# A planned one-core decoder block: a margin in the planner's costs, a later lower-bound computation, another order of filler columns

## The chip, the cores and the metric

The kernel runs on one core of a Trainium2 chip. The metric is the device time of one execution in microseconds. Beside the runs there is one profiled execution, whose trace gives every time quoted here unless a sentence says otherwise. The engines are called PE (matrix products), DVE (VectorE), ACT (ScalarE), POOL (GpSimd) and SP (it issues most DMAs).

## The reference

One decoder block on a 1024 x 1024 float32 activation, cut to what matters here:

```python
xn = rms_norm(x, norm1_g)
q, k, v, hq, hf, hi, hg, gate_sb, gate_hg = split(xn @ w_in)     # 1024 x 5632
o_sb = stick_breaking_attention(rms(q), rms(k), v)               # 8 heads of 64
f    = lb + (1 - lb) * sigmoid(hf)                               # lb: softmax of lb_table
o_hg = rms(hgrn2(silu(hq), f, hi)) * silu(hg)                    # 4 heads of 128
h    = x + (sigmoid(gate_sb) * (o_sb @ wb0) + sigmoid(gate_hg) * (o_hg @ wb1)) @ w_out
out  = h + (silu(rms(h) @ w_gate) * (rms(h) @ w_up)) @ w_down
```

Stick-breaking attention needs a reversed running sum of softplus over each row of scores; HGRN2 needs a running sum of log f and a decayed product between all pairs of rows. `lb` is a softmax over two rows of a table, 512 channels.

## The kernel before, in words

Activations lie transposed, channels on partitions, in two halves of 512 tokens. Products run at float32 accuracy on a reduced-precision path: each operand is split into a rounded part and a remainder (`ah`/`al` for activations, `oh`/`ol` for weights, `th`/`tl` for others), and three matmuls replace one. The rounded part is a copy on ACT or POOL, the remainder a subtraction on DVE.

The first stage computes the input projections and everything up to the branch outputs. There are four **units**: unit u is attention head pair u (`scores`, `values`) and HGRN head u (`hgrn`). A unit needs seven columns of 128 from `w_in` (q, k, v, hf, hq, hi, hg); sixteen more columns, called G, are the branch gates and wait for nobody. One column is 2 halves x 8 channel tiles x 3 = 48 matmuls of 128x512. The string list `FILL` says in which order the columns after the first six are projected while units 0 to 3 are worked on: a letter G is a gate column, `a` is the q, k, v of the next unit, the others are HGRN columns.

The order of nearly all instructions comes from a list scheduler inside the kernel, the class `Plan`. Every operation is recorded with a cost in us (`A` for ACT, `V` for DVE, `G` for POOL, `M` and `T` for PE, `L` for loads on SP), the operations it depends on and the buffers that it needs; `issue()` then plays the recorded operations on a clock of its own and writes them out, engine by engine, in the order in which they would start. A result can be used `max(FROM[producer], TO[consumer])` us after its producer's planned end, 0.14 us where no entry stands. `plan.at` gives a planned time before which an operation doesn't start. Projections have rank -1: they fill whatever PE time nothing else wants. On the chip each engine executes its own list strictly in the order written and waits on semaphores, so a wrong cost shows as a wait.

A score tile `z` is written by PE, then read by a chain on ACT (Abs, Relu, Exp, Ln into `aa` and `ww`) and DVE (a scan into `aa`, a subtraction into `ww`), after which its bank (two of them) is free for the next score tile. `vx` holds v, transposed on PE once DVE has scaled it. In `hgrn`, `kb` are key, running sum and the product matrix, `dl` the decayed operands of one level, and `sums` splits its operand on POOL (`th`) and DVE (`tl`) before PE sums it.

Names and lines of the kernel before: `setup` at L288 computes `lb` outside the planner; the first loads stand at L357 to L360; `WARM` matmuls on a constant at L378 run ahead of the first real ones; all planned instructions carry L204, the line at which `issue()` calls them, so they are told apart by their tiles. The output-branch, output and FFN stages that follow are planned too, with PE's order fixed by a chain; the last product (L1209) is written by hand.

Of the kernel before, what the change touches and what calls it, by code (L numbers as in the profile page):

```python
# [10 lines left out]
F32 = mybir.dt.float32  # L11
# [9 lines left out]
P = 128  # L21
# [8 lines left out]
LEVELS = [64, 32, 16, 8, 4, 2, 1]  # L30
FILL = ["GgGGaifq", "gGaGfiqGG", "gaGGGiqGfGG", "gGGG"]
BANKS = [3, 2, 3]
WARM = 9
ORDER = [1, 6, 2, 5, 7, 4, 3]
# [49 lines left out]
class Plan:  # L84
# [140 lines left out]
def hybrid_block(ctx: ExitStack, tc, xT, wi, wb, wo, wg, wu, wd, vec, outT):  # L225
# [62 lines left out]
    def setup(sp):  # L288
        make_identity(nc, ident)
        t2 = sp.tile([P, P], F32, tag="t2", name="t2")  # L290
        nc.vector.memset(t2, 0.0)
        nc.vector.memset(t2[0:64, 0:64], 1.0)
        nc.vector.memset(t2[64:128, 64:128], 1.0)
        nc.vector.tensor_copy(bones_r, t2)
        nc.vector.memset(never, NEG)

        for f, base, step in ((future[0], 0, -1), (future[1], 1 - P, 1)):
            nc.gpsimd.memset(f, 1.0)
            nc.gpsimd.affine_select(out=f, in_=f, pattern=[[1, P]], compare_op=ALU.is_ge, fill=0.0,
                                    base=base, channel_multiplier=step)  # L300
        nc.vector.tensor_scalar(qg, vt[:, V_Q:V_Q + 1], 0.125, None, op0=ALU.mult)
        l0, l1 = vt[:, V_LB:V_LB + 4], vt[:, V_LB + 4:V_LB + 8]
        mx = sp.tile([P, 4], F32, tag="mx", name="mx")
        e0 = sp.tile([P, 4], F32, tag="e0", name="e0")
        e1 = sp.tile([P, 4], F32, tag="e1", name="e1")
        nc.vector.tensor_tensor(mx, l0, l1, op=ALU.max)
        nc.vector.tensor_tensor(e0, l0, mx, op=ALU.subtract)
        nc.vector.tensor_tensor(e1, l1, mx, op=ALU.subtract)
        nc.scalar.activation(e0, e0, AF.Exp)
        nc.scalar.activation(e1, e1, AF.Exp)  # L310
        nc.vector.tensor_tensor(e1, e0, e1, op=ALU.add)
        nc.vector.reciprocal(e1, e1)
        nc.vector.tensor_tensor(lb, e0, e1, op=ALU.mult)
        nc.vector.tensor_scalar(omlb, lb, -1.0, 1.0, op0=ALU.mult, op1=ALU.add)
        nc.vector.tensor_scalar(nomlb, omlb, -1.0, None, op0=ALU.mult)

# [42 lines left out]
    nc.sync.dma_start(vt, vec)  # L359
    nc.sync.dma_start(first_w[0][0], first_src[0][:, :256])  # L360
    nc.scalar.preload_act_table_set("natural_log_exp_and_others")
# [90 lines left out]
    def fixed(tile):  # L452
        return Buf(None, lambda: tile)

    def A(fn, *args, n=HALF, aps=0, rank=0, ps=False, part=False, holds=(), after=(), **kw):
        us = (0.05 if ps else 0.093) + n / 1200 + 0.0935 * aps
        return plan.op("A", us, [(fn, args, kw)], rank, after, part=part, holds=holds)

    def V(fn, *args, n=HALF, aps=0, rank=0, part=False, holds=(), after=(), **kw):
        cycles = 2 * n if fn == nc.vector.tensor_tensor_scan else n  # L460
        us = 0.067 + cycles / 960 + 0.061 * aps
        return plan.op("V", us, [(fn, args, kw)], rank, after, part=part, holds=holds)

# [42 lines left out]
    def pool_copy(dst, src, rank=0, after=(), holds=()):  # L506
        return G(nc.gpsimd.tensor_scalar, dst, src, 1.0, 0.0, op0=ALU.mult, op1=ALU.add, us=0.68,
                 rank=rank, after=after, holds=holds)

    lvl_mask = []  # L510

    def level_masks():
# [5 lines left out]
        apart = fixed(apart)  # L518
        V(tt, apart, row, column, op=ALU.bitwise_xor, n=2 * P)
        for m in LEVELS:  # L520
# [28 lines left out]
    def first_piece(pieces, u, i):  # L549

        cut, src = slice(256 * i, 256 * i + 256), fixed(first_w[u][i])
        if i:
            load(src, first_src[u][:, cut], 128)
            hi, lo = (Buf(None, lambda b=b: b.buf.tile) for b in pieces[0])
            op = A(nc.scalar.copy, hi[:, cut], src, n=256, rank=2, holds=pieces[0])
        else:
            hi, lo = new("oh", dt=F32R), new("ol", dt=F32R)
            op = V(nc.vector.tensor_copy, hi[:, cut], src, n=128, rank=3)
            plan.at[op] = 2.3 + 0.3 * u
        V(tt, lo[:, cut], src, hi[:, cut].bitcast(F32), op=ALU.subtract, n=256, rank=3 - i)  # L560
        pieces.append((hi, lo))

    def take_x(h):
# [4 lines left out]
        for k in range(KT):  # L568
# [17 lines left out]
            if h == k == 0:  # L586
                plan.at[op] = 1.9
            V(stt, xl[k][h][:, hs(h)], x, g, xh[k][h][:, hs(h)].bitcast(F32), op0=ALU.mult,
              op1=ALU.subtract, aps=1, rank=2 - h)
            if k == 0:  # L590
                plan.at[A(act, acc, x, AF.Square, rank=1 - h)] = 1.9
            else:
                sq = new("ww")
                A(act, sq, x, AF.Square, rank=1 - h)
                sqs.append(sq)
# [8 lines left out]
    def proj(ws, h, after=None, ring="pj"):  # L604

        pss = [new(ring) for _ in ws]
        for k in range(KT):
# [693 lines left out]
```

## Time and profile before

| what | us |
|---|---|
| median of 3 runs (1499.06 to 1499.98) | 1499.16 |
| the profiled execution | 1496.39 |
| its span, first to last instruction | 1494.7 |
| PE busy | 1479.0 |
| DVE busy | 1193.1 |
| ACT busy | 806.5 |
| POOL busy | 92.3 |

A matmul's row shows 0.39 us from start to modelled end, though the next one starts 0.23 us after it: matmuls overlap. PE's busy time is the union of such rows, and a wait appears as idle time only where the previous row has ended. The time from the end of the span to the end of the execution, and what lies ahead of the span, is 1496.39 - 1494.7 = 1.69 us.

### The profile page before, as it was taken

What the parts mean: (1) busy time and instruction counts of PE and PEld (TensorE: products, weight loads), DVE (VectorE), ACT (ScalarE), POOL (GpSimd) and SP (SyncE); (2) the same over time, 40 slices, a digit from 0 to 9 for tenths busy, and PEclk for the clock granted to TensorE, in tenths of its full rate; (3) what the DMA queues carried; (4) which work ended last, traced back from release to release, by engine and by line L of the source; (5) the groups of instructions that cost most, each with busy time, mean ns of one, the idle gap of its engine ahead of it and who ended that gap; (6) DMA issues with size and microseconds to landing.
All of it is one profiled execution on the core that took longest, in us unless ns stands there. A gap on an engine that the chain in (4) does not pass through costs nothing.

```text
span 1494.7 us, 20135 instructions
## 1 busy us (share of the span) xinstructions
PE 1479.0 (99%) x7021; PEld 1224.2 (82%) x7021; DVE 1193.1 (80%) x2114; ACT 806.5 (54%) x1515; POOL 92.3 (6%) x131
## 2 busy tenths in 40 slices
PE   9999999999999999999999999999999999999999
PEld 7778888788878888888888888888888888888887
DVE  8899779988998678978867798888888888585553
ACT  8866868668757788546434453333333333354442
POOL 1111101211111001110000000000000000000000
PEclk9999999999999999999999999999999999999999
DMA  5011111111111211217434245444444445797662
GB/s 198 29 59 52 57 47 33 56 45 56 53 46 45 76 48 48 74 66 266 166 113 161 101 157 173 163 166 160 165 167 168 169 167 170 265 328 228 195 223 87
DMA packets 83445, 188.50 MB, mean 126 GB/s; under 512 B 9616, under 2 KB 12176, under 8 KB 83344
## 3 DMA queue, kind: packets, MB, share of 16 engines
q1 hardware_dynamic: 72688, 167.95, 33.7%
q10 hardware_dynamic: 10656, 19.27, 3.5%
q8 instruction: 55, 0.90, 0.2%
q14 instruction: 46, 0.38, 0.1%
HBM read 131.61 MB, written 55.57 MB: 125 GB/s over the span
## 4 chain that ended last, share of the span: by engine, by line
PE 81%; DVE 11%; ACT 5%; issue 2%; DMA 1%; POOL 1%; SPq 0%; POOLq 0%; DVEq 0%; ACTq 0%
PE pj L204 35%; PE ms L204 19%; PE f L1209 14%; PE z L204 13%; DVE dl L204 2%; DVE aa L204 2%; ACT aa L204 2%; DVE kb L204 1%; DVE ol L204 1%; DVE tail L204 1%; DVE tl L204 1%; ACT ww L204 1%; DVE ww L204 1%; ACT xf L204 1%; ACT qhh L204 0%
## 5 line engine op out<-in xcount | busy, mean ns | idle before, releaser
L204 PE MATMUL pj<-ah,oh 128*128 128x512 f32 x696 | 283.1, 407 | 0.5 <-DVE oh L204 0.5
L204 PE MATMUL pj<-ah,ol 128*128 128x512 f32 x696 | 272.7, 392 | 0.0
L204 PE MATMUL pj<-al,oh 128*128 128x512 f32 x696 | 271.9, 391 | 0.4 <-DVE al L204 0.3
L204 ACT CAST oh<-w 128x512 fp32r<-128x512 f32 x168 | 101.6, 620 | 236.0 <-PE ms L204 83.5
L204 DVE TENSOR_TENSOR ol<-w,oh 128x512 fp32r<-128x512 f32 x248 | 167.4, 690 | 10.6 <-ACT oh L204 8.3
L204 PE MATMUL ms<-f,oh 128*128 128x512 f32 x528 | 162.6, 389 | 0.2 <-DVE g L204 0.2
L204 PEld LDWEIGHTS pj<-ah,ol 128*128 128x128 f32 x696 | 130.6, 188 | 29.1 <-DVE ol L204 0.2
L204 PEld LDWEIGHTS pj<-al,oh 128*128 128x128 f32 x696 | 131.1, 189 | 23.6 <-DVE al L204 1.8
L204 PEld LDWEIGHTS pj<-ah,oh 128*128 128x128 f32 x696 | 131.2, 188 | 22.5 <-ACT ah L204 1.4
L204 PEld LDWEIGHTS ms<-f,oh 128*128 128x128 f32 x528 | 99.0, 188 | 21.1 <-DVE g L204 0.6
L1209 PE MATMUL f<-bl,ah 128*128 128x512 f32 x296 | 115.3, 389 | 0.0
L1209 PE MATMUL f<-bh,ah 128*128 128x512 f32 x296 | 115.2, 389 | 0.0
L1209 PE MATMUL f<-bh,al 128*128 128x512 f32 x296 | 115.2, 389 | 0.0
L204 DVE TENSOR_TENSOR_SCAN aa<-aa,ww 128x128 f32<-128x128 f32 (+3 forms) x96 | 93.7, 990 | 26.7 <-ACT aa L204 19.8
L204 PE MATMUL z<-f,oh 128*128 128x512 f32 x352 | 108.4, 389 | 0.0
L204 PE MATMUL pj<-f,oh 128*128 128x512 f32 x352 | 108.4, 389 | 0.0
L257 DVE TENSOR_TENSOR al<-ra,ah 128x512 fp32r<-128x512 f32 x73 | 50.5, 691 | 71.3 <-ACT ah L256 71.3
L204 PE MATMUL ms<-f,ol 128*128 128x512 f32 x264 | 102.7, 389 | 0.0
L256 ACT CAST ah<-ra 128x512 fp32r<-128x512 f32 x73 | 45.4, 622 | 94.6 <-PE f L1209 82.2
L204 POOL TENSOR_SCALAR oh<-w 128x512 fp32r<-128x512 f32 x80 | 64.4, 807 | 380.6 <-PE pj L204 311.9
L204 PE MATMUL pj<-mx,oh 128*128 128x512 f32 x256 | 78.8, 389 | 0.0
L204 PEld LDWEIGHTS pj<-f,oh 128*128 128x128 f32 x352 | 66.1, 188 | 13.6
(266 smaller groups left out, 3125.4 us busy)
## 6 DMA issues: line engine op xcount, KB each, us to landing
w<-wi SPq DMA_DIRECT2D x42, 512.0 KB, 3.6
rb<-act_d SPq DMA_DIRECT2D x73, 256.0 KB, 4.2
w<-wg SPq DMA_DIRECT2D x22, 512.0 KB, 3.6
w<-wu SPq DMA_DIRECT2D x22, 512.0 KB, 3.9
w<-wd SPq DMA_DIRECT2D x22, 512.0 KB, 4.7
wd_d<-ds SPq DMA_DIRECT2D x44, 256.0 KB, 2.7
ra<-wd_d SPq DMA_DIRECT2D x44, 256.0 KB, 4.0
act_d<-c SPq DMA_DIRECT2D x40, 256.0 KB, 4.5
```

The lines of the kernel that those rows point to most:

```text
L204: fn(*[a.real() if isinstance(a, View) else a for a in args], **{k: v.real() if isinstance(v, View) else v for k, v in kw.items()})
L256: pin(nc.scalar.copy(hi, src))
L257: pin(nc.vector.tensor_tensor(lo, src, hi.bitcast(F32), op=ALU.subtract))
L1209: nc.tensor.matmul(banks[SET[o]][d], l[:, ws], r, start=start and i == 0, stop=p == NP - 1 and i == 2, skip_group_check=True)
```

## The change

Five edits. (1) The planned cost of every ACT and DVE operation is multiplied by 1.02. (2) A result of POOL counts as usable 0.5 us after its planned end instead of 0.14, and POOL may start 0.24 us after its producer instead of 0.14. (3) The columns come in another order: with `a` as three, the four strings of `FILL` held 10, 11, 13 and 4 columns and now hold 11, 11, 10 and 6; there are sixteen G in both. (4) The ten small operations that compute `lb`, `omlb` and `nomlb` go from the hand-written beginning into the plan, with planned time 45 or later, and the operation that makes `apart` (for the level masks) gets planned time 40. (5) At the beginning, the load of the first weights becomes the first load of the plan, the rounded copy of the second column's first weights goes from DVE to ACT, there are 7 constant matmuls instead of 9, and the first matmuls are grouped otherwise.

```diff
-FILL = ["GgGGaifq", "gGaGfiqGG", "gaGGGiqGfGG", "gGGG"]
+FILL = ["GGgGaifqG", "gGaGGfiqG", "gaGiqGfG", "GgGGGG"]
-WARM = 9
+WARM = 7
-    FROM = {"P": 0.2, "D": 2.0}
-    TO = {"P": 0.35}
+    FROM = {"P": 0.2, "D": 2.0, "G": 0.5}
+    TO = {"P": 0.35, "G": 0.24}
...
-        l0, l1 = vt[:, V_LB:V_LB + 4], vt[:, V_LB + 4:V_LB + 8]
-        mx = sp.tile([P, 4], F32, tag="mx", name="mx")
...
-    nc.sync.dma_start(first_w[0][0], first_src[0][:, :256])
...
+    MARGIN = 1.02
     def A(fn, *args, n=HALF, aps=0, rank=0, ps=False, part=False, holds=(), after=(), **kw):
         us = (0.05 if ps else 0.093) + n / 1200 + 0.0935 * aps
-        return plan.op("A", us, [(fn, args, kw)], rank, after, part=part, holds=holds)
+        return plan.op("A", us * MARGIN, [(fn, args, kw)], rank, after, part=part, holds=holds)
...
-        return plan.op("V", us, [(fn, args, kw)], rank, after, part=part, holds=holds)
+        return plan.op("V", us * MARGIN, [(fn, args, kw)], rank, after, part=part, holds=holds)
...
+    lb, omlb, nomlb = (fixed(t) for t in (lb, omlb, nomlb))
+    def lower_bounds():
+        l0, l1 = vt[:, V_LB:V_LB + 4], vt[:, V_LB + 4:V_LB + 8]
+        plan.at[V(tt, omlb, l0, l1, op=ALU.max, n=4)] = 45.0
+        V(tt, lb, l0, omlb, op=ALU.subtract, n=4)
+        V(tt, nomlb, l1, omlb, op=ALU.subtract, n=4)
+        A(act, lb, lb, AF.Exp, n=4)
+        A(act, nomlb, nomlb, AF.Exp, n=4)
+        V(tt, omlb, lb, nomlb, op=ALU.add, n=4)
+        V(nc.vector.reciprocal, omlb, omlb, n=4)
+        V(tt, lb, lb, omlb, op=ALU.mult, n=4)
+        V(ts, omlb, lb, -1.0, 1.0, op0=ALU.mult, op1=ALU.add, n=4)
+        V(ts, nomlb, omlb, -1.0, None, op0=ALU.mult, n=4)
...
-        V(tt, apart, row, column, op=ALU.bitwise_xor, n=2 * P)
+        plan.at[V(tt, apart, row, column, op=ALU.bitwise_xor, n=2 * P)] = 40.0
...
+        if i or u == 0:
+            load(src, first_src[u][:, cut], 128)
         if i:
-            load(src, first_src[u][:, cut], 128)
...
-            op = V(nc.vector.tensor_copy, hi[:, cut], src, n=128, rank=3)
-            plan.at[op] = 2.3 + 0.3 * u
+            if u:
+                plan.at[A(nc.scalar.copy, hi[:, cut], src, n=256, rank=3)] = 2.6
+            else:
+                V(nc.vector.tensor_copy, hi[:, cut], src, n=128, rank=3)
...
-                groups = [a[:2] + b[:2], a[2:] + b[2:]]
+                groups = [a[:2], b[:1], a[2:] + b[2:], b[1:2]]
```

The new costs redraw the list of the whole first stage; what follows shows the written order at three places. In the names, a number behind a tile is its buffer; they differ between the two programs without meaning.

The first place is the beginning on DVE: the lower bounds (`mx` to `nomlb`), the mask operand `apart` and the first weights' rounded copies `oh`. Before:

```order
L301 TENSOR_SCALAR qg_89<-vt_66 128x1
L306 TENSOR_TENSOR mx_205<-vt_66 128x4
L307 TENSOR_TENSOR e0_206<-vt_66,mx_205 128x4
L308 TENSOR_TENSOR e1_207<-vt_66,mx_205 128x4
L311 TENSOR_TENSOR e1_207<-e0_206,e1_207 128x4
L312 RECIPROCAL e1_207<-e1_207 128x4
L313 TENSOR_TENSOR lb_90<-e0_206,e1_207 128x4
L314 TENSOR_SCALAR omlb_91<-lb_90 128x4
L315 TENSOR_SCALAR nomlb_92<-omlb_91 128x4
L204 TENSOR_TENSOR apart_243<-tmp_257,tmp_255 128x256
L204 CAST oh_265<-kb_177 128x256
L204 CAST oh_271<-kb_178 128x256
```

Now:

```order
L301 TENSOR_SCALAR qg_89<-vt_66 128x1
L204 CAST oh_249<-kb_177 128x256
L204 SCALAR_TENSOR_TENSOR al0_156<-tail_179,vt_66,ah0_155 128x512
L204 TENSOR_TENSOR ol_258<-kb_177,oh_249 128x256
L204 TENSOR_TENSOR ol_263<-kb_178,oh_251 128x256
L204 SCALAR_TENSOR_TENSOR al1_158<-aa_242,vt_66,ah1_157 128x512
```

Nine operations left the front of the first weights' copy, and one copy went to ACT.

The second place is on PE, where unit 0's v (`vx`) is transposed between the tiles of a projection. Before:

```order
L204 MATMUL pj_649<-ah5_165,oh_536 128x512
L204 MATMUL pj_649<-al5_166,oh_536 128x512
L204 MATMUL pj_649<-ah5_165,ol_544 128x512
L204 MATMUL ms_703<-ident_81,vx_607 128x128 x4
L204 MATMUL ms_710<-ident_81,vx_607 128x128 x4
L204 MATMUL pj_649<-ah6_167,oh_536 128x512
L204 MATMUL pj_649<-al6_168,oh_536 128x512
L204 MATMUL pj_649<-ah6_167,ol_544 128x512
```

Now:

```order
L204 MATMUL pj_634<-ah5_165,oh_520 128x512
L204 MATMUL pj_634<-al5_166,oh_520 128x512
L204 MATMUL pj_634<-ah5_165,ol_530 128x512
L204 MATMUL pj_634<-ah6_167,oh_520 128x512
L204 MATMUL pj_634<-al6_168,oh_520 128x512
L204 MATMUL pj_634<-ah6_167,ol_530 128x512
L204 MATMUL ms_696<-ident_81,vx_591 128x128 x4
L204 MATMUL ms_705<-ident_81,vx_591 128x128 x4
```

The transposes stand three matmuls later.

The third place is on DVE in unit 1's `hgrn`: `kb` (the product of key and query) is copied by POOL into `th`, and `tl` is the remainder, which waits for that copy. Before:

```order
L204 TENSOR_TENSOR xq_2755<-tmp_2790,xq_2755 128x512
L204 TENSOR_TENSOR ww_2783<-z_2731,aa_2835 128x512
L204 TENSOR_TENSOR kb_2869<-kb_2664,xq_2755 128x512
L204 TENSOR_TENSOR dl_2746<-xq_2755,dl_2746 128x256
L204 TENSOR_TENSOR dl_2761<-xq_2755,dl_2761 128x256
L204 TENSOR_TENSOR dl_2746<-dl_2746,kb_2664 128x2x2x64
L204 TENSOR_TENSOR tl_2892<-kb_2869,th_2880 128x512
```

Now, with the row that writes this `kb` (kb_2805) eight rows above the first one shown:

```order
L204 SCALAR_TENSOR_TENSOR aa_2851<-aa_2720,ww_2819 128x512
L204 SCALAR_TENSOR_TENSOR tmp_2828<-xq_2817,tmp_2828 128x512
L204 SCALAR_TENSOR_TENSOR aa_2866<-aa_2651,aa_2646,ww_2821 128x512
L204 TENSOR_TENSOR xq_2817<-tmp_2828,xq_2817 128x512
L204 TENSOR_TENSOR ww_2821<-z_2642,aa_2866 128x512
L204 TENSOR_TENSOR tl_2884<-ms_2784,th_2795 128x512
L204 TENSOR_TENSOR ww_2819<-z_2667,aa_2851 128x512
L204 TENSOR_TENSOR tl_2896<-ms_2808,th_2835 128x384
L204 TENSOR_TENSOR tail_2781<-tail_2781,xq_2740 128x512
L204 COPY_PREDICATED z_2900<-future0_84,never_86 128x128
L204 COPY state_2918<-ms_2904 128x128
L204 TENSOR_TENSOR tl_2925<-kb_2805,th_2909 128x512
```

Three operations stood between `kb` and its `tl`; now there are eighteen. Over the first stage's eight such pairs the mean goes from four to six, and for the last level's eight sums (`tl<-dl`) from two to four. From the output-branch stage on, PE's order is the same in both programs.

More of the change, by code (lines that the diff above doesn't have):

```diff
@@ L301, in setup @@
         nc.vector.tensor_scalar(qg, vt[:, V_Q:V_Q + 1], 0.125, None, op0=ALU.mult)
-        l0, l1 = vt[:, V_LB:V_LB + 4], vt[:, V_LB + 4:V_LB + 8]
-        mx = sp.tile([P, 4], F32, tag="mx", name="mx")
[L304 to L315, printed above, removed]
     COL = {"q": 0, "k": 4, "v": 8, "hq": 12, "hf": 16, "hi": 20, "hg": 24, "G": 28}
@@ L551, in first_piece @@
         cut, src = slice(256 * i, 256 * i + 256), fixed(first_w[u][i])
+        if i or u == 0:
+            load(src, first_src[u][:, cut], 128)
         if i:
-            load(src, first_src[u][:, cut], 128)
             hi, lo = (Buf(None, lambda b=b: b.buf.tile) for b in pieces[0])
-            op = A(nc.scalar.copy, hi[:, cut], src, n=256, rank=2, holds=pieces[0])
+            A(nc.scalar.copy, hi[:, cut], src, n=256, rank=2, holds=pieces[0])
         else:
             hi, lo = new("oh", dt=F32R), new("ol", dt=F32R)
-            op = V(nc.vector.tensor_copy, hi[:, cut], src, n=128, rank=3)
-            plan.at[op] = 2.3 + 0.3 * u
+            if u:
+                plan.at[A(nc.scalar.copy, hi[:, cut], src, n=256, rank=3)] = 2.6
+            else:
+                V(nc.vector.tensor_copy, hi[:, cut], src, n=128, rank=3)
         V(tt, lo[:, cut], src, hi[:, cut].bitcast(F32), op=ALU.subtract, n=256, rank=3 - i)
@@ L586, in take_x @@
             if h == k == 0:
-                plan.at[op] = 1.9
+                plan.at[op] = 2.0
             V(stt, xl[k][h][:, hs(h)], x, g, xh[k][h][:, hs(h)].bitcast(F32), op0=ALU.mult,
@@ L590, in take_x @@
             if k == 0:
-                plan.at[A(act, acc, x, AF.Square, rank=1 - h)] = 1.9
+                plan.at[A(act, acc, x, AF.Square, rank=1 - h)] = 2.1
             else:
@@ L899, in hybrid_block @@
             take_x(1)
+            lower_bounds()
             level_masks()
```

## The prediction

> **What bounds the kernel now.** I read the page's busy shares first, then the windows by stage, then who made PE wait, then the timeline around three of those waits.
>
> ```profile
> span 1494.7 us, 20135 instructions
> PE 1479.0 (99%) x7021; PEld 1224.2 (82%) x7021; DVE 1193.1 (80%) x2114; ACT 806.5 (54%) x1515; POOL 92.3 (6%) x131
> ```
>
> PE is the bound: 15.7 us of the span are left beside its busy time. A window's row gives, after the stretch and its length, each engine's busy time; PE comes first, then weight loads, DVE, ACT, POOL.
>
> ```profile
> 0.00:10.00 10.00, 8.04 (x23) 5.36 (x23) 6.95 (x29) 6.73 (x13) 4.02 (x15) 1.00 0.80 267
> 10.00:50.00 40.00, 39.23 (x171) 30.90 (x170) 36.89 (x62) 36.20 (x64) 1.92 (x2) 1.00 0.34 119
> 50.00:250.00 200.00, 198.07 (x1023) 165.45 (x1024) 173.10 (x338) 155.69 (x325) 27.84 (x37) 1.00 0.16 50
> 250.00:450.00 200.00, 195.10 (x1029) 162.19 (x1028) 178.79 (x365) 137.00 (x276) 31.51 (x39) 1.00 0.16 49
> 450.00:690.00 240.00, 237.90 (x1256) 199.81 (x1255) 188.64 (x344) 172.46 (x349) 27.05 (x39) 1.00 0.24 83
> 690.00:1490.00 800.00, 799.71 (x3522) 660.06 (x3521) 608.03 (x979) 298.45 (x492) 0.00 (x0) 1.00 0.52 176
> ```
>
> PE stands idle 1.96 us in the first 10, 0.77 to 50, then 1.93, 4.90 and 2.10 us, 8.93 in all from 50 to 690. After 690 it is 0.29 us in 800. So only the first stage has anything to give, and its worst stretch is the one where DVE is fullest (178.79 of 200). Who ended the waits:
>
> ```profile
> PE z L204 <- DVE ww L204: 3.4, 5, 1.1
> PE ms L204 <- DVE kb L204: 2.9, 6, 0.8
> PE ms L378 <- DVE ones_r L365: 1.4, 1, 1.4
> PE ms L204 <- DVE vx L204: 1.0, 1, 1.0
> PE ms L204 <- DVE tl L204: 0.8, 2, 0.5
> PE ms L204 <- DVE ot L204: 0.4, 1, 0.4
> PE ms L204 <- ACT ww L204: 0.4, 1, 0.4
> ```
>
> Nearly all are DVE being late by a few tenths, 16 waits of some 0.55 us in these rows from 50 on. The largest:
>
> ```profile
> 431.69 0.39 PE L204 MATMUL pj<-al,oh 128*128 128x512 f32 x1
> 431.92 0.39 PE L204 MATMUL pj<-ah,ol 128*128 128x512 f32 x1
> 433.42 0.50 PE L204 MATMUL z<-khl,qhh 128*128 128x512 f32 x1 [1.11 <-DVE ww L204]
> ```
>
> Matmuls follow each other by 0.23 us, so this one was due at 432.15 and started 1.27 late: the idle time shown, 1.11, hides 0.16 more, since the row of the one before runs on to its modelled end. The 16 waits therefore cost about 8.9 + 16 x 0.16 = 11.5 us.
>
> **The beginning (edits 4 and 5).**
>
> ```profile
> 3.08 0.23 DVE L306 TENSOR_TENSOR mx<-vt 128x4 f32<-128x4 f32 x1
> 5.33 0.42 DVE L204 TENSOR_TENSOR apart<-tmp 128x256 int32<-128x256 int32 x1
> 5.70 0.50 DVE L204 CAST oh<-kb 128x256 fp32r<-128x256 f32 x2
> 1.72 0.42 SPq L360 DMA_DIRECT2D kb<-wi  x1
> 6.14 0.54 PE L204 MATMUL pj<-ah,oh 128*128 128x512 f32 x1 [0.48 <-DVE oh L204]
> 6.58 0.50 PE L204 MATMUL pj<-ah,ol 128*128 128x512 f32 x1
> L378 PE MATMUL ms<-ones_r 128*128 128x512 f32 x9 | 4.2, 647 | 1.4 <-DVE ones_r L365 1.4
> ```
>
> From 3.08 to 5.7 DVE works on the lower bounds and the mask, and the copy that PE waits for stands behind them. With these gone, the weights themselves decide; the copy has no idle time before it, so they had landed by 5.7. Their load is issued third on SP, behind 256 KB of x; at the 267 GB/s of the first window those 256 KB take 1.0 us, so as first load its data come about that much earlier, near 4.7, and x a half us later, 128 KB. Nine constant matmuls take 4.2 us, seven some 3.3 and end near 4.8. The first real one can start at about 5.0 instead of 6.14: 1.1 us. [...]
>
> Not all of it lasts, since DVE and ACT are 92% and 90% busy from 10 to 50:
>
> ```profile
> 15.97 1.32 ACT L204 ACTIVATE ah<-xf,vt 128x512 fp32r<-128x512 f32 x2
> 17.36 0.74 DVE L204 SCALAR_TENSOR_TENSOR al<-xf,vt,ah 128x512 fp32r<-128x512 f32 x1
> 19.43 0.51 PE L204 MATMUL pj<-al,oh 128*128 128x512 f32 x1 [0.29 <-DVE al L204]
> ```
>
> ACT's work here follows loads that the change doesn't hasten, so the first `ah<-xf` stays near 16.0 and ends near 16.6; its `al` can start 0.7 earlier than 17.36 at best. PE, 1.1 ahead, waits 0.4 more at 19.43: I keep 0.7. Ten small operations come back near 45 us, at 0.16 each about 1.3 us of DVE, beside masks and under projections; three of them stand ahead of the last `vx` piece:
>
> ```profile
> 50.53 0.44 PE L204 MATMUL ms<-ident,vx 128*128 128x128 f32 x2 [0.97 <-DVE vx L204]
> ```
>
> The transposes moved three matmuls back, 0.68 us, and DVE has 0.3 to 0.5 more ahead of `vx`: 0.2 of this wait goes. Together -0.9; bounds +0.5 (the x tile's half us decides) and -2.1 (1.1 kept, all of the 0.97 gone).
>
> **The costs (edits 1 and 2).** How wrong were the planner's costs? It charges a 512-wide subtraction 0.067 + 512/960 = 0.600 us, and a projection's three matmuls 1536/2255 + 0.009 = 0.690.
>
> ```profile
> 29.34 0.69 DVE L204 TENSOR_TENSOR tl<-aa,th 128x512 fp32r<-128x512 f32 x1
> 29.94 0.69 DVE L204 TENSOR_TENSOR tail<-tail,ww 128x512 f32<-128x512 f32 x1
> ```
>
> DVE starts one every 0.60, as charged. PE does three in 0.68 (431.69 to 431.92 is 0.23 each), 1.3% faster than charged. So over a stretch in which DVE has no pause, PE runs ahead of the plan and meets a DVE that is on time for the plan, late for PE. A DVE cost 2% higher lets it be late by 2% of such a stretch: over 10 to 15 us, 0.2 to 0.3. Taking 0.25 from each of 16 waits of 0.72 gives 4.0 at most; short waits have less to give, so 3.3.
>
> Other lateness comes from POOL:
>
> ```profile
> 249.35 1.33 POOL L204 TENSOR_SCALAR th<-kb 128x512 fp32r<-128x512 f32 x1 [4.39 <-PE z L204]
> 249.79 0.42 DVE L204 TENSOR_TENSOR dl<-dl,kb 128x256 f32<-128x256 f32 x1
> 250.72 0.69 DVE L204 TENSOR_TENSOR tl<-kb,th 128x512 fp32r<-128x512 f32 x1 [0.51 <-POOL th L204]
> 255.42 0.71 PE L204 MATMUL ms<-dl 128*128 128x128 f32 x4 [0.65 <-DVE kb L204]
> ```
>
> DVE stood 0.51 for a POOL copy and PE waited 0.65 five us later. The planner charges that copy 0.07 + 512/840 = 0.68 us; it took 1.33. With 0.36 more allowed for, DVE's `tl` stands eighteen operations behind `kb` instead of three. If two or three of the six `kb` waits go by this, it is 1.0 us. Sum: -4.3.
>
> This redraws the whole list, so the bounds come from the stretches: at the rate of the worst one (4.90 in 200) the 640 us would idle 15.7 us, 6.8 more than now; nothing better than none, -11.5.
>
> **The columns (edit 3)** move no work: 48 matmuls of 0.23 are 10.9 us a column in either order, and PE never lacked filler before 690. 11, 11, 10, 6 spreads what covers the four units' DVE work more evenly than 10, 11, 13, 4. I put it at nothing, inside the same bounds; without cover in the last unit, the 450 to 690 stretch would lose more than its 2.10. The later stages keep PE's order; their 0.29 us bounds a gain, a new late DVE operation there would cost as much.
>
> Sum: -0.9 - 4.3 = -5.2; on the profiled execution 1496.39 - 5.2 = 1491.2. The runs' median, 1499.16, is 2.8 above it, so 1494.0 is predicted. About 0.2%, 3 us, is what a measurement tells from no change.
>
> **Rivals.** *The list trades its waits one for one.* All DVE and ACT costs grow by the same factor, so their order among themselves needn't change, and a new draw has new tight places. For it: 0.25 is less than half of a typical wait. Against: filler is always at hand, so planned slack costs PE nothing. Only the beginning's 0.9 stays: 1498.3.
>
> *POOL is held off longer.* The chip's POOL copy doesn't take a fixed time:
>
> ```profile
> 86.44 2.02 POOL L204 TENSOR_SCALAR oh<-w 128x512 fp32r<-128x512 f32 x1 [3.70 <-PE pj L204]
> 87.30 0.67 DVE L204 TENSOR_TENSOR ol<-w,oh 128x512 fp32r<-128x512 f32 x1
> 88.49 0.69 DVE L204 TENSOR_TENSOR ol<-w,oh 128x512 fp32r<-128x512 f32 x1 [0.52 <-POOL oh L204]
> L204 POOL TENSOR_SCALAR th<-kb 128x512 fp32r<-128x512 f32 x8 | 5.9, 743 | 23.3 <-DVE kb L204 13.3 <-PE ms L204 5.6 <-PE z L204 4.4
> ```
>
> It ended 0.5 after DVE fell idle, here and at 250.72, as if it had to wait for DVE. If so, operations put between `kb` and `tl` only push the copy's end along, the sums come later, and PE, which now expects them, waits. From seven of sixteen on (eight `kb`, eight `dl`) the gain is eaten; if twelve cost PE 0.51 + 0.16 each, 8.0 stands against 0.9 and 3.3: 1503.0. Against it: five of the twelve DVE rows shown ahead of the new `tl` read `ms` or `z`, not two tiles of the kind that stood beside the long copies. [...]
>
> *The drift was nearly all of it.* If PE's 1.3% and DVE's latencies are all that made it late, most of the 11.5 us goes: 1499.16 - 0.9 - 9 = 1489.3. For it: the fullest stretch waits most. Against: single waits of 1.1.
>
> **How the numbers follow.** Forecast, a gain of 2.5 to 8: 0.57, of which 0.52 beyond 3 us. One for one: 0.21, all within 3 us. POOL: 0.13, of which 0.11 slower by over 3. Nearly all: 0.09. So faster 0.61, same 0.28, slower 0.11. The forecast's own range is 1491 to 1496.7. For 8 in 10 I go down to 1488.5, nearly all of the drift case, and up to 1500.5, over the one-for-one case and the near half of POOL's.
>
> **What would show it.** First real matmul near 5.0, with the PE idle of 0 to 10 below 1.6. PE idle from 50 to 690 near 5.5 instead of 8.93; fewer than 12 waits on `ww` and `kb`, shorter than 0.5 on average. DVE's waits for POOL fewer; `th<-kb` near 743 ns on average would say that the copies aren't held off longer, 1000 that they are. It is wrong if the first stage's idle time stays above 8, or if PE's waits after 690 grow beyond a microsecond.

## The result, and the profile after

| | before | after | difference |
|---|---|---|---|
| median of the runs, us | 1499.57 (4 runs, 1499.06 to 1500.36) | 1485.62 (4 runs, 1484.21 to 1487.79) | -13.95 |
| the profiled execution, us | 1496.39 | 1485.27 | -11.12 |

The ratio is 0.9912, 95% interval 0.99 to 0.9924. The change made the kernel faster, as forecast, but by 13.95 us where 5.2 were forecast, and 1485.62 lies below the range (1488.5 to 1500.5). The two rows differ by 2.8 us because before's profiled execution was 3.2 us faster than the median of its runs, and after's only 0.35. The sets of 13 to 25 runs of the kernel before that stand beside the experiments below have medians of 1498.29 to 1498.76; against those the gain is some 13 us.

The page of the kernel after opens with:

```profile
span 1483.6 us, 20109 instructions
PE 1473.9 (99%) x7019; PEld 1224.1 (83%) x7019; DVE 1190.3 (80%) x2113; ACT 807.1 (54%) x1516; POOL 99.1 (7%) x131
```

PE is still the bound, with 9.7 us of the span beside its busy time (15.7 before). The windows of the kernel after, with the columns of the prediction's (PE first):

```profile
0.00:10.00 10.00, 7.89 (x22) 4.94 (x23) 5.88 (x20) 6.61 (x12) 4.03 (x15) 1.00 0.74 244
10.00:50.00 40.00, 39.60 (x173) 31.18 (x172) 37.42 (x66) 36.74 (x67) 1.80 (x2) 1.00 0.36 127
50.00:250.00 200.00, 197.87 (x1020) 164.90 (x1021) 173.03 (x342) 155.01 (x324) 30.18 (x36) 1.00 0.16 51
250.00:450.00 200.00, 199.78 (x1075) 169.25 (x1074) 177.85 (x357) 154.38 (x321) 29.66 (x38) 1.00 0.17 54
450.00:690.00 240.00, 239.53 (x1259) 202.03 (x1258) 201.13 (x375) 163.90 (x314) 33.45 (x40) 1.00 0.27 91
690.00:1480.00 790.00, 789.18 (x3477) 651.85 (x3475) 594.45 (x958) 290.49 (x483) 0.00 (x0) 1.00 0.52 175
```

From 50 to 690 PE stands idle 2.13, 0.22 and 0.47 us, 2.82 in all, against 8.93. The worst stretch before, 250 to 450, went from 4.90 to 0.22. Who ends the waits now:

```profile
PE ms L363 <- DVE ones_r L350: 1.4, 1, 1.4
PE z L204 <- DVE ww L204: 1.2, 3, 0.8
PE pj L204 <- DVE al L204: 0.5, 2, 0.3
PE ms L204 <- DVE tl L204: 0.4, 1, 0.4
PE f L1217 <- ACT bh L256: 0.4, 1, 0.4
PE ms L204 <- DVE kb L204: 0.4, 2, 0.2
PE pj L204 <- DVE oh L204: 0.3, 1, 0.3
PE ms L204 <- DVE vx L204: 0.2, 1, 0.2
```

`ww` went from 5 waits and 3.4 us to 3 and 1.2, `kb` from 6 and 2.9 to 2 and 0.4: of the eleven, six are gone, and the five that are left are shorter (0.3 on average, 0.6 before).

To see the delays that show no idle time as well, I add up over successive PE rows how much later than the usual distance (0.227 us for a matmul of 512 columns, 0.118 for 256, 0.109 for 128) the next one starts; a wait counts in the stretch of the row ahead of it. This **lateness of PE** splits the 11.1 us of the profiled executions:

| stretch, us | before | after | difference |
|---|---|---|---|
| 0 to 50 | 6.44 | 5.83 | -0.6 |
| 50 to 650 | 23.38 | 14.04 | -9.3 |
| 650 to 720 | 0.99 | -0.01 | -1.0 |
| behind 720 | 0.54 | 0.81 | +0.3 |

The sum is -10.7 before rounding; the remaining 0.45 are the two constant matmuls fewer (7019 PE rows instead of 7021, 2 x 0.227). So nearly everything came from the list of the first stage, 10.3 us where the prediction had 4.3. The experiments ask which part of the change did it.

### The profile page after: what moved, and what is told of

It is laid out like the page before. It is cut to its first block, busy times and chain, and to the rows that moved or that the text cites. A ratio compares the mean times of both kernels' runs of the same rounds, so it can differ in the third digit from the quotient of the medians.

```text
span 1483.6 us, 20109 instructions
## 1 busy us (share of the span) xinstructions
PE 1473.9 (99%) x7019; PEld 1224.1 (83%) x7019; DVE 1190.3 (80%) x2113; ACT 807.1 (54%) x1516; POOL 99.1 (7%) x131
## 4 chain that ended last, share of the span: by engine, by line
PE 82%; DVE 12%; ACT 3%; issue 1%; DMA 1%; POOL 0%; SPq 0%; ACTq 0%; DVEq 0%; POOLq 0%
PE pj L204 38%; PE ms L204 18%; PE f L1217 14%; PE z L204 13%; DVE dl L204 2%; DVE aa L204 2%; ACT aa L204 1%; DVE kb L204 1%; DVE ol L204 1%; DVE tl L204 1%; DVE ww L204 1%; DVE tail L204 1%; ACT qhh L204 1%; DVE g L204 0%; DVE xg L204 0%
## 5 line engine op out<-in xcount | busy, mean ns | idle before, releaser
L204 DVE TENSOR_TENSOR_SCAN aa<-aa,ww 128x512 f32<-128x512 f32 (+3 forms) x96 | 93.2, 981 | 18.0 <-ACT ww L204 9.4
L204 POOL TENSOR_SCALAR oh<-w 128x512 fp32r<-128x512 f32 x80 | 68.6, 858 | 376.9 <-PE pj L204 309.0
L204 PEld LDWEIGHTS z<-f,oh 128*128 128x128 f32 x352 | 66.1, 188 | 13.7
```

The source lines that it names most:

```text
L204: fn(*[a.real() if isinstance(a, View) else a for a in args], **{k: v.real() if isinstance(v, View) else v for k, v in kw.items()})
```

## The experiments

Three terms for what follows. **Ordinary waits** are PE's idle time from 50 to 650 without single waits of over 1.4 us; such a single wait is called a **hole**. The **hand-over** is the passage to the output-branch stage near 685: its first product reads `o`, which ACT and DVE make out of the loads `ld<-o_d`, and these wait for the stores of the last values product (`ms<-tl,vv`).

### One part undone

The kernel after without the margin, without POOL's latencies, with the old columns, and with the old beginning:

```diff
u_margin (against after)
-    MARGIN = 1.02
+    MARGIN = 1.0
u_pool (against after)
-    FROM = {"P": 0.2, "D": 2.0, "G": 0.5}
-    TO = {"P": 0.35, "G": 0.24}
+    FROM = {"P": 0.2, "D": 2.0}
+    TO = {"P": 0.35}
u_fill (against after)
-FILL = ["GGgGaifqG", "gGaGGfiqG", "gaGiqGfG", "GgGGGG"]
+FILL = ["GgGGaifq", "gGaGfiqGG", "gaGGGiqGfGG", "gGGG"]
u_begin (against before: margin, latencies and columns, old beginning)
-FILL = ["GgGGaifq", "gGaGfiqGG", "gaGGGiqGfGG", "gGGG"]
+FILL = ["GGgGaifqG", "gGaGGfiqG", "gaGiqGfG", "GgGGGG"]
-    FROM = {"P": 0.2, "D": 2.0}
-    TO = {"P": 0.35}
+    FROM = {"P": 0.2, "D": 2.0, "G": 0.5}
+    TO = {"P": 0.35, "G": 0.24}
+    MARGIN = 1.02
-        return plan.op("A", us, [(fn, args, kw)], rank, after, part=part, holds=holds)
+        return plan.op("A", us * MARGIN, [(fn, args, kw)], rank, after, part=part, holds=holds)
-        return plan.op("V", us, [(fn, args, kw)], rank, after, part=part, holds=holds)
+        return plan.op("V", us * MARGIN, [(fn, args, kw)], rank, after, part=part, holds=holds)
```

> The change with the margin taken back to 1.0 (POOL's latencies, columns and beginning stay). Drift theory (PE runs 1.3% faster than charged, DVE is late for it, the margin makes up for that): most of the 6.1 us of PE idle time that went between 50 and 690 comes back, 4 to 6 us slower than the changed kernel, about 1490.5. Column theory (the margin matters little, the columns do): within 1.5 us of 1485.6. Draw theory (any new list has its own tight places): anywhere from 1484 to 1494, with waits at other places.

> The change with POOL's two latencies taken out (margin, columns and beginning stay). Drift theory: 1 us slower than the changed kernel at most, 1486.5. POOL theory (the copies' lateness was the larger part): 4 us slower or more, 1490, with DVE's waits for POOL back and PE waits on kb near the 2.9 us of before. Draw theory: 1484 to 1494.

> The change with the old order of columns (10, 11, 13, 4). Drift theory: within 1.5 us of the changed kernel, 1485.6 to 1487. Column theory: 4 us slower or more, 1490, with the idle time back between 250 and 450, where it was 4.90 us before and is 0.22 now. Draw theory: 1484 to 1494.

> The kernel before with margin, POOL's latencies and the new columns, but the old beginning (lower bounds first, weights third, 9 constant matmuls). All theories: the first real matmul at 6.1 again instead of 5.1. If the lead lasts, 1 us slower than the changed kernel, 1486.6; if ACT and DVE eat it before 50 us, the same within 0.5. Draw theory: up to 4 us either way from waits further on.

Measured, beside 1498.29 us for the kernel before (25 runs): u_margin 1498.29 (ratio 1.0, 0.9991 to 1.0009), u_pool 1506.73 (1.0053, 1.0038 to 1.0068), u_fill 1497.43 (0.9995, 0.9986 to 1.0005), u_begin 1501.53 (1.0021, 1.0012 to 1.0031). Undoing any one part takes the whole gain away, even the beginning. Shares can't be read from that: four parts can't each be worth 12 to 21 us of 14. Nor were these times foretold: the highest figure that any of the theories named was 1494, and all four kernels lie above it. The traces tell what happened instead. The kernel without POOL's latencies, windows of the first stage and of the hand-over:

```profile
50.00:650.00 600.00, 595.53 (x3125) 499.84 (x3126) 512.03 (x1013) 436.71 (x898) 85.11 (x113) 1.00 0.17 53
650.00:720.00 70.00, 58.18 (x262) 45.65 (x261) 48.71 (x69) 41.65 (x65) 0.62 (x1) 0.90 0.48 165
```

Up to 650 it is nearly as good as the change (4.5 us idle); 11.8 us are idle at the hand-over, and the granted clock is 0.90 on average there. Three views of the same kernel, of SP's loads, of ACT and of PE:

```profile
681.09 2.01 SPq L204 DMA_DIRECT2D ld<-o_d  x4
```

```profile
685.18 1.04 ACT L204 CAST o<-ld 128x1024 fp32r<-128x1024 f32 x1 [5.12 <-DMA ld<-o_d]
```

```profile
679.39 0.27 PE L204 MATMUL ms<-tl,vv 128*128 128x128 f32 x1
686.28 0.80 PE L204 MATMUL pj<-o,oh 128*128 128x512 f32 x1 [6.62 <-ACT o L204]
```

The last values product starts at 679.39, PE has nothing more to do, and store, load and copy take until 686.28. The kernel after has the same chain, but projections over it. Its PE rows:

```profile
653.83 0.28 PE L204 MATMUL ms<-tl,vv 128*128 128x128 f32 x1
...
674.21 0.39 PE L204 MATMUL pj<-ah,ol 128*128 128x512 f32 x1
674.43 0.62 PE L204 MATMUL pj<-o,oh 128*128 128x512 f32 x2
```

From 653.83 to 674.43 PE works without a gap, 20.6 us in which the eight loads come in and all but the last are copied. In the kernel with the old columns the loss is a hole. Its PE rows, and the window around:

```profile
271.33 0.28 PE L204 MATMUL ms<-tl,vv 128*128 128x256 f32 x1
277.65 0.80 PE L204 MATMUL z<-khl,qhh 128*128 128x512 f32 x1 [6.04 <-DVE ww L204]
```

```profile
250.00:450.00 200.00, 193.50 (x1022) 162.81 (x1021) 178.03 (x360) 140.68 (x285) 30.75 (x39) 0.97 0.16 49
```

No projection stands between 271.33 and 277.65 in its written order, so a wait for one DVE result is bare; of the 6.5 us idle in this window it is 6.04. The idle time between 250 and 450 is back, as the column theory had it, but in one piece that the old list did not have. The lists of u_margin and u_begin have, in turn, a hole of 2.27 us and 4.6 us idle at the hand-over. So the redraw itself brings losses as large as the gain.

### One part alone

```diff
o_margin (against before): the two "us * MARGIN" lines, MARGIN = 1.02
o_fill (against before): the new FILL
o_pool (against before): the "G" entries of FROM and TO
o_begin (against after): MARGIN = 1.0, old FILL, no "G" entries
pe_true (against before), a truer PE in place of slower others
-cols / 2255 + 0.003 * len(mms)
+cols / 2255
v_only, a_only (against after): the margin on VectorE's or on ScalarE's operations only; v_only's
-        return plan.op("A", us * MARGIN, [(fn, args, kw)], rank, after, part=part, holds=holds)
+        return plan.op("A", us * 1.0, [(fn, args, kw)], rank, after, part=part, holds=holds)
```

> The kernel before with the margin of 1.02 alone. Drift theory: PE's idle time from 50 to 650 falls by 5 to 6 us from 8.9, and since 14.3 us of projections still stand behind the last values matmul (15.0 before), nothing is lost at the hand-over to the next stage: 1492.5. If the margin is worth something only together with the columns: 1498 within 2.

> The kernel before with PE's planned cost lowered to what the trace shows (512/2255 = 0.227 us a matmul, without the 0.003 more), no margin. Drift theory: this takes away the 1.3% by which PE outruns the plan, so about two thirds of what the margin brings, 4 us: 1494.5. Slack theory (the margin helps because it allows for variation, not for drift): within 1.5 us of 1498.3. Work behind the last values matmul is 14.3 us, as with the margin alone.

> The kernel before with the new order of columns alone; 22.5 us of projections stand behind the last values matmul instead of 15.0. Drift theory: ordinary waits stay near 8.9 us of PE idle time from 50 to 650; the hand-over was not on the path before (0.25 us at 690), so 1498.3 within 2. Column theory: the waits of 250 to 450 go, 1493.

> The kernel before with the changed beginning alone (lower bounds and mask operand late, first weights as first load, one copy on ACT, seven constant matmuls): no margin, old GpSimd costs, old column order. The written order has the kernel before's 15.0 us of cover and its one planned hole, 1.0 us at 409. Theory: first real matmul near 5.1 us, from 50 us on the waits of the kernel before, 8 to 10 us from 50 to 650; 0.3 to 1.2 us less than the kernel before, 1497.3 to 1498.3 us. Rival (the beginning is worth more than the prediction's 0.9, since every later wait is measured from it): 3 us or more less, under 1495.5.

> The kernel before with GpSimd's two latencies alone (FROM and TO entries of G); no margin, old columns, old beginning. The planner's own clock has a hole here, 3.0 us and several of 0.4 to 1.5 between 111 and 129, which the kernel before has not; 14.3 us of work behind the last values product. Theory (the latencies do nothing for PE by themselves, since it was not waiting for GpSimd's copies): outside the stretch from 105 to 135, PE's idle time from 50 to 650 is 7 to 10 us, as before; with the hole 4 to 8 us more: 1500 to 1506 us. Rival (the prediction's term): outside that stretch 1 us or more less than the kernel before's 9.3, and fewer waits on kb.

> The changed kernel with the margin of 1.02 on VectorE's costs alone (ScalarE's as before). Its written order has 2.0 us of other work behind the last values product (20.5 in the changed kernel), so a bare hand-over is expected whatever the theory: a PE wait of 3 to 6 us near 685, 6 to 11 us idle from 650 to 720, and the half clock behind it; 1498 to 1507 us. What tells the theories apart is PE's idle time from 50 to 650: if VectorE's lateness was the cause, 2.5 to 4.5 us; if ScalarE's was, 8 us or more, as without a margin.

> The changed kernel with the margin of 1.02 on ScalarE's costs alone (VectorE's as before). 10.2 us of work behind the last values product. If VectorE's lateness was the cause, PE's idle time from 50 to 650 stays at 7 to 10 us, with DVE as the one waited for in most of it; if ScalarE's was, 2.5 to 4.5 us. At the hand-over 2 to 5 us idle. 1494 to 1500 us by the first, 1488 to 1493 by the second.

Measured:

| kernel | median, us | ratio to before, 95% interval |
|---|---|---|
| o_margin | 1490.95 | 0.9947 (0.9932 to 0.9962) |
| pe_true | 1497.10 | 0.9991 (0.9982 to 1.0) |
| o_fill | 1493.31 | 0.9962 (0.9948 to 0.9976) |
| o_begin | 1498.14 | 0.9997 (0.9988 to 1.0006) |
| o_pool | 1505.18 | 1.0042 (1.0029 to 1.0055) |
| v_only | 1504.46 | 1.0036 (1.0023 to 1.0049) |
| a_only | 1499.77 | 1.0009 (1.0 to 1.0019) |

The kernel before had medians of 1498.29 to 1498.76 us beside them, in 13 to 25 runs each time.

With these, all eight combinations of margin, POOL's latencies and columns have a trace (before, o_margin, o_fill and o_pool with the old beginning, u_margin, u_fill, u_pool and after with the new one). The idle time of PE from 50 to 650 in each, as its windows row gives it (600 less PE's busy time), the hole in it, and what is left:

| | POOL old, columns old | POOL new, columns old | POOL old, columns new | POOL new, columns new |
|---|---|---|---|---|
| no margin | before: 8.9 | o_pool: 9.6 - 3.0 = 6.6 | o_fill: 5.6 | u_margin: 11.0 - 2.3 = 8.7 |
| margin 1.02 | o_margin: 2.7 | u_fill: 9.9 - 6.0 = 3.9 | u_pool: 4.5 | after: 2.8 |

The rows of three of them, from the windows of o_margin, of o_fill and of u_margin:

```profile
50.00:650.00 600.00, 597.29 (x3148) 500.34 (x3147) 524.07 (x1025) 447.36 (x922) 91.20 (x113) 1.00 0.17 53
```

```profile
50.00:650.00 600.00, 594.44 (x3127) 495.66 (x3127) 526.11 (x1027) 447.18 (x924) 82.42 (x112) 1.00 0.17 53
```

```profile
50.00:650.00 600.00, 588.98 (x3095) 491.34 (x3094) 522.28 (x1030) 446.76 (x918) 85.02 (x111) 1.00 0.16 52
```

Every list with the margin has fewer ordinary waits than every list without: 3.5 us on average against 7.4 (4.0 apart before rounding). Counting every gap, however short, there are 17 waits against 26.5; of those over 0.15 us, the kind of the prediction's 16, there are 7.75 against 16. **The margin is worth 4.0 us of idle time.** As lateness from 50 to 650, which sees delays without idle time too, it is worth more. In the order of the table, with each hole, the 0.16 us that it hides and half of the stretch at half clock behind it (an estimate, last section) taken out, the lists without the margin have 23.4, 20.1, 20.2 and 24.4 us and those with it 16.1, 14.3, 17.2 and 14.0: 22.0 against 15.4, 6.6 us. The beginning isn't balanced over the eight: three of the four lists with the margin have the new one, and one of the four without. That doesn't make the difference: with u_begin (5.05 us of ordinary waits) and o_begin (8.6) added, the margin takes 3.1 us off the lists with the old beginning and 4.9 off those with the new one.

POOL's latencies give -2.3, +1.1, +3.2 and -1.7 in the four pairs, +0.1 on average; the columns -3.3, +2.2, +1.8 and -1.0, -0.1 on average; as lateness, -1.0 and +0.5. Neither can be told from zero, since single pairs differ by 1 to 4 us either way. Single runs mislead here: o_fill alone met the column theory (1493.31 where 1493 was expected, and the idle time from 250 to 450 fell from 4.90 to 1.25); o_pool taken alone, with 5.4 us of PE waits outside the stretch from 105 to 135 where before had 9.0, would have spoken for the latencies, and the pair u_margin and o_fill against them.

pe_true goes at the same drift from the other side: without the 0.003 us per matmul PE's plan runs at its real pace. Its ordinary waits are 4.7 us, as few as in the lists with the margin, beside a hole of 3.98 us and 1.6 us idle at the hand-over, with a granted clock of 0.997 on average over the run (1.0 in the kernel before). So its time, 1497.10, is within 1.5 us of 1498.3, as the slack theory had it, and decides nothing; its waits speak for the drift, in one list. The two halves of the margin, windows of v_only and then of a_only:

```profile
50.00:650.00 600.00, 595.11 (x3132) 499.74 (x3131) 521.60 (x1023) 442.75 (x910) 86.57 (x113) 1.00 0.17 53
650.00:720.00 70.00, 60.78 (x264) 46.87 (x263) 44.06 (x62) 37.21 (x56) 0.62 (x1) 0.90 0.47 167
```

```profile
50.00:650.00 600.00, 593.07 (x3118) 496.00 (x3119) 515.09 (x1021) 442.73 (x912) 87.60 (x113) 1.00 0.17 53
650.00:720.00 70.00, 67.87 (x315) 54.50 (x314) 52.27 (x76) 39.95 (x58) 0.62 (x1) 0.98 0.53 188
```

On VectorE alone 4.9 us are left (4.89, a little over the 4.5 expected of that theory), on ScalarE alone 6.9 (7.2 with the part of the first wait that lies ahead of 50), inside the range of the lists without a margin. So it seems to be mainly VectorE's lateness that the margin takes out; with one list each that isn't shown, and ScalarE's share stays open. v_only loses the gain at the hand-over (9.2 us), as its written order foretold.

o_begin is the beginning by itself: 0.6 us in the medians, inside what can be told from none.

### The same change with another margin

```diff
m1021, m1015, m10125, m10225 (against after)
-    MARGIN = 1.02
+    MARGIN = 1.021    (1.015, 1.0125, 1.0225)
```

> The change with 1.021 for 1.02. In its list the last projection stands 3.1 us of PE work before the last values matmul, where the change has 20.5 us behind it. Hand-over theory: the loads of the next stage come too late, PE idles some 8 us near 680 and its clock falls, as in the run without POOL's latencies; ordinary waits stay as low as in the change (3 us of idle time from 50 to 650): 1485.6 + 15 = 1500. If the change's time is robust: 1486 within 2.

> The changed kernel with a margin of 1.015 in place of 1.02, nothing else. Counted from the written order, PE has 21.2 us of projections behind the last values product (20.5 in the changed kernel), and on the planner's own clock PE never stands idle between 50 and 720 us. Theory (ordinary waits are set by the costs; what is lost beside them is lost in holes of the written order and at the hand-over to the next stage): PE idle 2.3 to 4 us from 50 to 650, none above 1.5 at one place, under 0.5 at the hand-over, granted clock never below 1; 1483 to 1487 us. Rival (a redraw of the list is a draw that nothing in it foretells; the six redrawn lists so far lay between 1491 and 1513): anywhere from 1487 to 1513.

> The changed kernel with a margin of 1.0125, nothing else. 21.8 us of projections behind the last values product, one planned hole of 0.4 us at 103. Theory: as for the margin of 1.015, a few tenths more: PE idle 3 to 5 us from 50 to 650, under 0.5 at the hand-over; 1483.5 to 1488 us. Rival: anywhere from 1487 to 1513.

> The changed kernel with a margin of 1.0225, nothing else. Counted from the written order, all projections stand ahead of the last values product, with 4.4 us of other work between (-4.4 us of cover), and the planner's own clock has holes of 0.95 us at 103 and 0.55 at 282. Theory: the loads of the values for the next stage lie bare, a PE wait of 5 to 8 us near 690 and smaller ones beside it, 9 to 13 us idle from 650 to 720, and a granted clock of half for 10 to 20 us behind it; ordinary waits of 3 to 5 us from 50 to 650; 1504 to 1512 us. Rival (the gain grows smoothly with the margin): within 2 us of the changed kernel's 1485.6.

| margin | median, us | ratio to before, 95% interval | ordinary waits | hole | idle 650 to 720 |
|---|---|---|---|---|---|
| 1.0 (u_margin) | 1498.29 | 1.0 (0.9991 to 1.0009) | 8.7 | 2.3 | 0.0 |
| 1.0125 | 1490.96 | 0.9946 (0.993 to 0.9963) | 5.3 | - | 0.0 |
| 1.015 | 1487.26 | 0.9925 (0.991 to 0.994) | 3.4 | - | 0.0 |
| 1.02 (after) | 1485.62 | 0.9912 (0.99 to 0.9924) | 2.8 | - | 0.0 |
| 1.021 | 1513.22 | 1.0095 (1.008 to 1.011) | 4.9 | 4.4 | 10.9 |
| 1.0225 | 1508.78 | 1.007 (1.0055 to 1.0085) | 4.7 | - | 12.2 |

A tenth of a per cent more margin makes the kernel 27.6 us slower. Where it goes, from the PE rows of the kernel with 1.021:

```profile
511.98 0.79 PE L204 MATMUL z<-khl,qhh 128*128 128x512 f32 x1 [4.37 <-DVE ww L204]
...
691.30 0.80 PE L204 MATMUL pj<-o,oh 128*128 128x512 f32 x1 [6.23 <-ACT o L204]
```

One hole and a bare hand-over. The expectation foresaw the hand-over and missed the hole: 1500 where 1513.22 was measured. Both can be read before a run. The hand-over is covered by the PE work that stands behind the last values product; the trace's counterpart is the time from that product to the first `pj<-o`:

| kernel | last values product | first product of the next stage | between | idle 650 to 720 |
|---|---|---|---|---|
| after | 653.8 | 674.4 | 20.6 | 0.0 |
| m1015 | 655.5 | 676.8 | 21.3 | 0.0 |
| o_fill | 659.6 | 682.2 | 22.6 | 0.0 |
| before | 670.2 | 685.4 | 15.2 | 0.1 |
| o_margin | 662.5 | 677.0 | 14.5 | 1.8 |
| a_only | 671.1 | 681.6 | 10.4 | 2.1 |
| u_begin | 671.3 | 678.9 | 7.7 | 4.6 |
| v_only | 675.8 | 683.1 | 7.4 | 9.2 |
| u_pool | 679.4 | 686.3 | 6.9 | 11.8 |
| m10225 | 683.2 | 690.1 | 6.9 | 12.2 |
| m1021 | 684.8 | 691.3 | 6.5 | 10.9 |

With 20 us between them nothing is lost, at 15 it is on the edge (o_begin, whose list from 50 on is nearly that of the kernel before, also has 15.2 and lost 1.7; o_pool and pe_true with 14.5 lost 2.1 and 1.6), at 7 to 8 it costs 5 to 12. The total of PE's work in the stage is fixed, so what differs is how late the last unit's chain comes. Holes stand in the planner's own times, too: PE's planned pauses of 6.2 us in u_fill, 4.5 in m1021, 3.9 in pe_true, 3.0 in o_pool and 2.55 in u_margin came as 6.04, 4.37, 3.98, 2.98 and 2.27. The bare hand-over is planned as well: played over again, the planner puts the first product of the next stage at 651.5 us of its own clock with the margin of 1.02 and at 669.8 with 1.021. So these losses stand in the order itself.

That was put to the test with the three margins 1.015, 1.0125 and 1.0225, whose expectations were written from the lists alone. The bare hand-over of 1.0225 came as said: 1508.78 of 1504 to 1512, 12.2 us idle of 9 to 13. The windows of that kernel:

```profile
650.00:720.00 70.00, 57.84 (x256) 45.55 (x256) 47.24 (x70) 43.17 (x71) 0.00 (x0) 0.85 0.42 148
```

The margin of 1.015 has no hole and a covered hand-over: 1487.26, 0.26 us above the range expected. At 1.0125 holes and hand-over are as foretold, but 1490.96 is 3 us above its range: more ordinary waits were left than I had allowed for (5.3 us where 3 to 5 were expected). Both times also lie in the range of the rival, a draw that nothing foretells (1487 to 1513), so it is the idle times, and 1.0225, that speak for the theory. The written order tells whether a list loses 5 us and more, not its last 3 us. None of the fifteen kernels tried beats the change.

## Why the prediction was right in direction and wrong in size

**The beginning, -0.9.** The sum is right within what can be measured: lateness up to 50 fell by 0.6 in the trace, the two constant matmuls make it 1.06, and o_begin is 0.6 us faster, which can't be told from nothing. PE's timeline after:

```profile
4.17 0.63 PE L363 MATMUL ms<-ones_r 128*128 128x512 f32 x1
5.08 0.71 PE L204 MATMUL pj<-ah,oh 128*128 128x512 f32 x1 [0.27 <-DVE oh L204]
5.98 0.50 PE L204 MATMUL pj<-ah,ol 128*128 128x512 f32 x1 [0.19 <-DVE ol L204]
```

The first real matmul starts at 5.08, as forecast (5.0). The split of the sum was wrong, and its size partly luck: the sixteenth real matmul starts only 0.45 us earlier than before, and at 43 us 0.33 is left of the 0.7 that was to be kept; `vx` costs 0.2 where it cost 0.97, a gain of 0.7 where 0.2 was put. Nor is that one the beginning's alone, since o_margin, with the old beginning, has no such wait either. The mark "PE idle of 0 to 10 below 1.6" was wrong, at 2.11: the two constant matmuls that were taken out had counted as busy, and PE now waits for `oh` and `ol`.

**The margin, -3.3.** The direction is right, the drift behind it is borne out by pe_true and v_only in one list each, and the size was off by half: 6.6 us of lateness. The step that failed is "Taking 0.25 from each of 16 waits ... short waits have less to give, so 3.3", with the 11.5 us that it started from. Those 11.5 were the idle time with 0.16 us hidden in each of 16 waits. PE's lateness from 50 to 650 was twice that, 23.4 us, since a delay of under 0.16 us shows no idle time at all; and over the eight lists the waits over 0.15 us did not lose 0.25 each but went from 16 to 7.75. Why a 2% allowance undoes that much is open: the step took the stretch over which DVE falls behind as 10 to 15 us, and 4.0 us over the 9.5 gaps that went is 0.42 for each, which would take a stretch of some 21 us (0.42 / 0.02), an estimate that no run tested. Its marks came true and were overshot: 5 waits on `ww` and `kb` where fewer than 12 were named, 2.82 us idle from 50 to 690 where 5.5 was. The rival "one for one" fell with this, and so did its reason: the order of DVE's work against PE's is what the factor changes.

**POOL's latencies, -1.0.** Not confirmed: +0.1 us of idle time and -1.0 of lateness on average of four pairs, with 2 to 4 us of spread. The step that failed is the reading of one case, a copy that ended late with a `kb` wait five us behind it, as the cause of the `kb` waits: with the margin alone `kb` no longer appears among o_margin's waits of 0.2 us or more, without any change to POOL. Over the eight lists these waits come to 1.05 us with the latencies and 1.3 without. Of the eight pairs of `kb` and `tl` only the one that the prediction looked at moved by more than two operations. What the latencies may have shortened is DVE's own waiting for POOL, 3.3 us on average against 5.7, most of that from u_pool's 10.3, and PE did not gain by it. The rival that POOL is held off longer looks half right in the changed kernel. The copies of `kb`, the group's row on the page after, mean 966 ns behind the bar (743 before):

```profile
L204 POOL TENSOR_SCALAR th<-kb 128x512 fp32r<-128x512 f32 x8 | 7.7, 966 | 31.0 <-PE ms L204 14.0 <-ACT aa L204 8.5 <-ACT ww L204 5.7
```

That is near the 1000 named as the mark. But the latencies aren't its cause: with them alone (o_pool) the mean is 622, without them in pe_true 966, and over the eight lists it is 803 with and 705 without, single lists lying between 622 and 1000. How long the copies take goes with the list. And DVE's waits for POOL, first before and then after, hardly moved in sum:

```profile
DVE tl L204 <- POOL th L204: 2.4, 8, 0.5
DVE ol L204 <- POOL oh L204: 2.1, 4, 0.6
```

```profile
DVE tl L204 <- POOL th L204: 3.5, 4, 1.8
DVE ol L204 <- POOL oh L204: 0.5, 1, 0.5
```

4.5 us in 12 waits became 4.0 in 5, and of PE's waits only 0.4 us are left on `kb`. What failed in that rival is its last step, that PE would wait for the later sums.

**The columns, nothing.** Right on average (-0.1), and wrong in its reason: "PE never lacked filler before 690" holds for the list of the kernel before, not for its neighbours. u_fill stood 6.04 us and o_pool 2.98 without any.

**The redraw.** The prediction bounded the new list by idle rates of the old one (-11.5 to +6.8) and put the likely end at the sum of the terms. What it did not price was the cover of the hand-over and the holes, although the order of the changed kernel was there to be counted: 20.5 us of PE work behind the last values product against 15.0. On the fifteen kernels a hole cost 2 to 6 us of waiting and a bare hand-over 5 to 12, the half clock behind them not counted (below). After's list has neither, and its ordinary waits are among the lowest. That is luck as far as these runs show: nothing in the five edits makes sure of it, and u_pool, u_fill, u_begin and the margin of 1.021 are its near neighbours. Its lateness from 50 to 650 fell by 9.3 us, of which 6.1 show as idle time, and 1.0 more went at the hand-over. So of the 11.1 us in the trace some 6.6 are the margin's, 1.1 came by 50 us, and the remaining 3.4 belong to this particular list. Why the planner's rules give this list at 1.02 and a much worse one at 1.021 is left open.

**The step from the trace to the median.** I added 2.8 us because before's profiled execution stood that far below its runs. After's stood 0.35 below its own: 2.4 of the 8.4 us by which 1494.0 missed. The larger sets of the kernel before put its median near 1498.5, so that some 0.7 of these 2.8 were the first set's. Of the 8.4, then, 3.3 are the margin's size, 3.4 this list, 2.4 this step and 0.2 the beginning, less the 1.0 put down to POOL's latencies.

## What to carry to other kernels

Where a planner orders the work, any edit of its costs redraws the list, and one pair of lists doesn't tell what the edit is worth: here the lists differed by 28 us for a tenth of a per cent, so the effect (4 us of waits, 6.6 of lateness) showed only over eight lists with and without it. Before a run, count two things in the new order, the PE work that covers each passage between stages (15 to 20 us were wanted here) and every place where PE has nothing written to fill a wait. Then correct the cost that is off against the trace (here PE's three matmuls in 0.68 us, charged 0.69; pe_true did that alone, and lost the gain again to a hole), and try several neighbouring values rather than one. A forecast of what waits can give back should start from the lateness of the bound engine, not from its idle time: here 23.4 us against 8.9.

## What the runs showed of the hardware

I had not expected the granted clock to fall in an otherwise full PE. In the kernel with POOL's latencies alone (o_pool), PE's rows and the window behind the hole:

```profile
122.74 0.69 PE L204 MATMUL z<-khl,qhh 128*128 128x384 f32 x1 [2.98 <-DVE ww L204]
123.22 0.52 PE L204 MATMUL z<-khl,qlz 128*128 128x384 f32 x1
123.61 0.80 PE L204 MATMUL z<-khl,qhh 128*128 128x512 f32 x1
124.20 0.63 PE L204 MATMUL z<-khl,qlz 128*128 128x512 f32 x1
```

```profile
121.90:132.10 10.20, 8.07 (x28) 6.61 (x29) 9.32 (x26) 6.82 (x14) 0.40 (x1) 0.51 0.18 51
```

After 2.98 us of waiting, the two matmuls of 512 columns start 0.59 us apart, and the granted clock is 0.51 on average over 10.2 us. (In u_pool, where it is 0.50 from 697.00 to 700.40, two such matmuls start 0.43 us apart, at 698.31 and 698.74, instead of 0.23.) In the other kernels with a hole of 4 us and more it was also below 1: 0.97 on average over 250 to 450 in u_fill, around 6.04 us of waiting, and 0.97 over 450 to 550 in m1021, around 4.37 us. In u_margin, with 2.27 us of waiting, the average over the run is 1.0. But the length of the wait doesn't sort these runs. In u_begin (0.995 over the run) PE was idle for 1.37 us of the 3.41 us ahead of the fall, and 13.65 us at 0.50 followed:

```profile
680.69:684.10 3.41, 2.04 (x7) 0.97 (x6) 3.25 (x4) 3.00 (x4) 0.00 (x0) 1.00 1.03 417
684.10:697.75 13.65, 11.04 (x22) 5.94 (x21) 12.47 (x17) 8.60 (x9) 0.00 (x0) 0.50 0.70 282
```

What decides when the clock falls, and for how long, is left open here.

I count such a stretch at half its length. That is an estimate from o_pool: its PE waits add up to 14.24 us against 10.51 before, 3.7 more, and half of 10.2 is 5.1, together 8.8 of the 9.2 us by which its span is longer. By the same estimate the clock adds to the price of a bare hand-over: m10225's is 0.85 on average over the 70 us from 650 to 720, which is 10.5 us (0.15 x 70) beside its 12.2 us of idle time.
